# Sums of squares and residuals by adding DMA transfers instead of GpSimd additions, in an RG-LRU / gMLP / conv-FFN block

## The chip, the cores and the metric

The kernel runs on one core of a Trainium2 chip. The metric is the device time of one execution in microseconds, lower is better. Engines are named as the profile names them: PE (TensorE), DVE (VectorE), ACT (ScalarE), POOL (GpSimd), SP (SyncE, which here only issues DMA transfers).

## The reference

One residual block over 2048 positions of width 1024, in f32. A mixer and a feed-forward network each have the same frame: RMS norm, scale and shift from a conditioning vector, the layer, RMS norm, gate, residual.

```
h = rmsnorm(x, g_mix_pre) * (1 + sc_m) + sh_m
z = h @ w_in                       # lru_x | lru_gate | g_u | g_v
y_lru  = rg_lru_group(lru_x, lru_gate, ...)
y_gmlp = gmlp_group(g_u, g_v, ...)
y = concat(rmsnorm(y_lru), rmsnorm(y_gmlp)) @ w_out
x = x + gt_m * rmsnorm(y, g_mix_post)
h = rmsnorm(x, g_ffn_pre) * (1 + sc_f) + sh_f
up = causal_depthwise_conv(h @ w_up)      # width 3
y = (gelu(up_g) * up_v) @ w_down
x = x + gt_f * rmsnorm(y, g_ffn_post)
```

Each rmsnorm needs a mean of squares over the 1024 channels of a position: `x * rsqrt(mean(x*x) + EPS) * g`.

## The kernel before, in words

Channels lie on the 128 partitions (8 blocks of them), positions along the free axis. The mixer goes over four chunks c = 0 to 3 of 512 positions, the FFN over two halves C of 1024. A tile `[128, 2, 512]` (512 KB) holds two channel blocks of a chunk, so a chunk is four tiles, j = 0 to 3. Matmuls are done as three products of float32r parts (`mm3`, L177 to L179, and `prod`, L971 to L973), and `split` (L136 to L141) makes the two parts.

A mean of squares is built by the class `SumSq`: ACT squares a tile (L215), POOL adds it to the first one (L219), `done` adds the two halves on DVE (L223) and splits the sum (L140, L141); `rms_bcast` multiplies it with a matrix of 1/1024 on PE (L199), so that every partition has the mean, and ACT and DVE make the reciprocal root (L202, L203). It is used at these places:

- `x_rms` (tiles `n_s`): the norm ahead of the mixer, chunks 1 to 3, three additions each.
- `norm_scale` (`rl_s`, `rg_s`): the norms of the two halves of y, all four chunks, one addition each.
- `mixer_out` (`rp_s`): the product with `w_out`, evicted to `oo`, squared, all chunks, three additions each.
- `mixer_post` (chunks 0 and 1) and `late_post` (chunks 2 and 3), tiles `rq_s`: scale by gate and norm on DVE (L604, L583), load the chunk's x as `xr` through the pool `ld` of three buffers, add it (on POOL at L605, on DVE at L584), store to `x2d` in DRAM (SP), square, three additions each.

`late_post` runs late, beside the FFN's first products, and takes its input back from `o2d` in DRAM. Background work is written as generators in the list `bg`; `tick` advances each by one step between pieces of PE work, and `wait` inserts empty steps. All of this fixes a priority for each instruction; the framework's planner then simulates the engines (`schedule_with_timeline_sim=True`) and fixes the order of each engine's instructions. On the chip every engine, and the issuing queues of SP, ACT and POOL, run their own list in order, with semaphores between them.

Other work on POOL: weight splits in the first chunks (L141), storing split weights to DRAM (`kept`, L169, transfers issued by POOL), products in the LRU (L380, L503), and from the first FFN half on the additions that make the seven weight pieces of `up_weights` (L951 to L959, `wt`), which feed ACT and DVE splits and then PE.

Of the kernel before, what the change touches and what calls it, by code (L numbers as in the profile page):

```python
# [13 lines left out]
ALU = mybir.AluOpType  # L14
# [26 lines left out]
def block_kernel(ctx: ExitStack, tc: tile.TileContext, xt, cols, rows, wada, wada_r, win_k, win_s, win_v, wgate, wsp, wout, wup, wdown, out):  # L41
# [12 lines left out]
    vec, act, pool, pe, sync = nc.vector, nc.scalar, nc.gpsimd, nc.tensor, nc.sync  # L54

    def t4(name):
        return tp.tile([P, 2, 512], F32, tag="t4", name=name)
# [39 lines left out]
    def start(*gens):  # L97
        bg.extend(gens)
        return gens

    def wait(n):
        for _ in range(n):
            yield
# [25 lines left out]
    x2d = dram.tile([NFC, P, ND, FT], F32, name="x2d")  # L129
# [59 lines left out]
    def rms_split(ssum, name, n=512):  # L189
        with tc.high_priority(offset=100):  # L190
            shl = y4(f"{name}_hl")
            split(shl[:, 0, :n], shl[:, 1, :n], ssum, "dve")
        return shl

    def rms_bcast(shl, scale, name, tag="r2", bufs=2, n=512):

        pt = bank(f"{name}_m")
        for q in range(2):
            pe.matmul(out=pt[:, :n], lhsT=onesD, rhs=shl[:, q, :n], start=(q == 0), stop=(q == 1))  # L199
        r = rp.tile([P, 512], F32, tag="r", name=f"{name}_r")  # L200
        with tc.high_priority(offset=100):
            act.activation(out=r[:, :n], in_=pt[:, :n], func=AF.Sqrt, scale=scale, bias=epst)  # L202
            vec.reciprocal(out=r[:, :n], in_=r[:, :n])  # L203
        return r

    class SumSq:


        def __init__(self, name, eng=None):
            self.acc, self.name, self.n, self.eng = None, name, 0, eng or pool  # L210

        def add(self, t):
            s = t4(f"{self.name}_s{self.n}")
            self.n += 1
            act.activation(out=s, in_=t, func=AF.Square)  # L215
            if self.acc is None:
                self.acc = s
            else:
                self.eng.tensor_tensor(out=self.acc, in0=self.acc, in1=s, op=ALU.add)  # L219

        def done(self):
            a = self.acc
            vec.tensor_tensor(out=a[:, 0], in0=a[:, 0], in1=a[:, 1], op=ALU.add)  # L223
            return rms_split(a[:, 0], self.name)

    def load_x(src, c, j, name, mk=None):
        x = mk(f"{name}_{j}") if mk else lp.tile([P, 2, 512], F32, tag="ld", name=f"{name}_{j}")
        sync.dma_start(out=x, in_=src[c // 2, :, 2 * j:2 * j + 2, (c % 2) * 512:(c % 2) * 512 + 512])
        return x

    rx = {}
# [2 lines left out]
    def x_rms(c, late=2):  # L234
        q = SumSq(f"n{c}")
        for j in range(4):
            q.add(load_x(xt, c, j, f"xq{c}"))
            yield
        yield
        hl = q.done()  # L240
        yield from wait(late)
        rx[c] = rms_bcast(hl, 1.0, f"n{c}", "rr", 4)

    def build_h(src, c, hl, s, sh, name):
        hi, lo = hl
        r = rx[c]
        for j in range(4):
            x = load_x(src, c, j, name)
            hi.append(h4(f"{name}hi{j}"))
            lo.append(h4(f"{name}lo{j}"))  # L250
            for b in range(2):
                d = 2 * j + b
                vec.scalar_tensor_tensor(out=x[:, b], in0=x[:, b], scalar=s[:, d:d + 1], in1=r, op0=ALU.mult, op1=ALU.mult)
                act.activation(out=hi[j][:, b], in_=x[:, b], func=AF.Identity, bias=sh[:, d:d + 1])
            for b in range(2):
                d = 2 * j + b
                vec.scalar_tensor_tensor(out=lo[j][:, b], in0=x[:, b], scalar=sh[:, d:d + 1], in1=hi[j][:, b].bitcast(F32), op0=ALU.add, op1=ALU.subtract)
            yield
# [288 lines left out]
    def mixer_out(c, late=False):  # L547
        Yt = Y[c]
        O = []
        q = SumSq(f"rp{c}")  # L550
        for j in range(4):
            pt = psum(f"o{c}_{j}")
            for b in range(2):
                wh, wl = weight_once(("o", 2 * j + b), wout[2 * j + b], [P, 8, P], f"wout{c}_{j}_{b}", pool if b else vec)
                for k in range(8):
                    mm3(pt[:, b], (wh[:, k], wl[:, k]), (Yt[k // 2][0][:, k % 2], Yt[k // 2][1][:, k % 2]), k == 0, k == 7)
                tick()
            o = t4(f"oo{c}_{j}")
            act.copy(out=o, in_=pt)
            q.add(o)  # L560
            if late:
                sync.dma_start(out=o2d[c - 2, :, j], in_=o)
            else:
                O.append(o)
        return O, q
# [8 lines left out]
    def late_post(c):  # L574

        r = rlate[c]
        q = SumSq(f"rq{c}")
        for j in range(4):
            x = load_x(xt, c, j, f"xr{c}")
            o = t4(f"ol{c}_{j}")  # L580
            sync.dma_start(out=o, in_=o2d[c - 2, :, j])
            for b in range(2):
                vec.scalar_tensor_tensor(out=o[:, b], in0=o[:, b], scalar=gm[:, 2 * j + b:2 * j + b + 1], in1=r, op0=ALU.mult, op1=ALU.mult)  # L583
            vec.tensor_tensor(out=o, in0=o, in1=x, op=ALU.add)  # L584
            sync.dma_start(out=x2d[c // 2, :, 2 * j:2 * j + 2, (c % 2) * 512:(c % 2) * 512 + 512], in_=o)
            q.add(o)
            yield
        hl = q.done()
        yield
        rq[c] = hl  # L590
# [3 lines left out]
    def mixer_post(c, O, q):  # L594
        yield
        hl = q.done()
        yield from wait(2)
        r = rms_bcast(hl, 1.0, f"rp{c}")
        q = SumSq(f"rq{c}")
        for j in range(4):  # L600
            x = load_x(xt, c, j, f"xr{c}")
            for b in range(2):
                o = O[j][:, b]
                vec.scalar_tensor_tensor(out=o, in0=o, scalar=gm[:, 2 * j + b:2 * j + b + 1], in1=r, op0=ALU.mult, op1=ALU.mult)  # L604
            pool.tensor_tensor(out=O[j], in0=O[j], in1=x, op=ALU.add)  # L605
            sync.dma_start(out=x2d[c // 2, :, 2 * j:2 * j + 2, (c % 2) * 512:(c % 2) * 512 + 512], in_=O[j])
            q.add(O[j])
            yield
        yield
        hl = q.done()  # L610
        yield from wait(6)
        rx[c] = rms_bcast(hl, 1.0, f"rq{c}", "rr", 4)
# [199 lines left out]
    for c in range(1, NC):  # L812
        nt = start(mixer_norm(0) if c == 1 else norm_split(c - 1))
        xr = start(x_rms(c + 1, 8)) if c + 1 < NC else ()
        mixer_z(c)
        drain(*xr, *nt)
        if c == 1:
            m3, = start(ada_task(3, 1))
        if c == 2:
            m4, = start(ada_task(4, 1))  # L820
        if c + 1 < NC:
            ht = start(h_task(c + 1, False), norm_scale(c, 3))
            O, q = mixer_out(c - 1)
            drain(*ht)
            if c == 1:
                drain(m2)
                vec.tensor_tensor(out=gm, in0=modc[:, 16:24], in1=colr("g_mix_post", 0, 8), op=ALU.mult)
            start(mixer_post(c - 1, O, q))
# [290 lines left out]
    def late_chunks():  # L1119

        yield from late_rms(NC - 1, q3)
        for c in (NC - 2, NC - 1):
            yield
            yield from late_post(c)
            yield
            rx[c] = rms_bcast(rq[c], 1.0, f"rq{c}")
# [5 lines left out]
    O, q = mixer_out(NC - 2, True)  # L1132
# [3 lines left out]
    O, q3 = mixer_out(NC - 1, True)  # L1136
# [91 lines left out]
```

## Time and profile before

| | |
|---|---|
| median of 3 runs | 2222.09 us (2219.21 to 2222.97) |
| the profiled execution | 2222.2 us, its span 2220.4 us |
| mean granted TensorE clock | 0.971 |
| instructions | 24098 |
| mixer and `late_post` | from the start to about 950 us |
| FFN, first half `down` and second half | about 1200 us to the end |

The span runs from the first to the last instruction; the profiled execution's time is 1.8 us longer. The granted clock is a share of TensorE's full speed of 2.4 GHz; it has two levels, 1 and 0.5 (1.2 GHz), and a mean between them says how much of a stretch was spent at each. A busy time is the time in which an engine had an instruction running. An instruction that is held by something else while it runs counts as busy, and shows as a longer duration.

### The profile page before, as it was taken

To read this page: it belongs to the slowest core of one execution; us is meant where nothing else is said; L and a number is where in the kernel's file an instruction comes from. 1 tells how busy PE (TensorE), PEld (TensorE's weight loads), DVE (VectorE), ACT (ScalarE), POOL (GpSimd) and SP (SyncE) were. 2 spreads that over 40 slices of the span, in tenths; PEclk is the share of its full clock that TensorE was granted. 3 is DMA by queue.
4 is the path that set the end of the run, shared out by engine and by line. 5 is a ranking of instruction groups with operands and counts; after the bars stand their busy time and mean duration, and the time that the engine had idled before them with its cause. 6 is when DMAs were issued, how large, how long until landed. Compare 5 with 4: busy or idle time off the path is not lost.

```text
span 2220.4 us, 24098 instructions
## 1 busy us (share of the span) xinstructions
PE 2072.0 (93%) x9032; PEld 1700.7 (77%) x9032; DVE 1435.9 (65%) x1598; ACT 928.8 (42%) x1154; POOL 424.8 (19%) x248
## 2 busy tenths in 40 slices
PE   5898969999998998799999999989999999999995
PEld 4686858888877876588888888868888888888883
DVE  7788789795766887898777437474444444533634
ACT  3472733534635544355555344343233332422422
POOL 4454243234203332443320000020000000000000
PEclk9999989999999999899999999999999999999997
DMA  8587568587674887877775546537666666444541
GB/s 315 187 311 286 193 242 291 206 287 256 225 268 164 305 314 265 311 264 276 271 291 189 181 134 215 173 120 286 220 221 224 220 223 221 145 159 149 212 148 60
DMA packets 157748, 501.14 MB, mean 226 GB/s; under 512 B 15296, under 2 KB 15424, under 8 KB 157632
## 3 DMA queue, kind: packets, MB, share of 16 engines
q1 hardware_dynamic: 149568, 470.25, 59.9%
q0 software_dynamic: 6912, 25.17, 2.9%
q10 hardware_dynamic: 1152, 4.19, 0.5%
q8 instruction: 71, 1.16, 0.2%
q14 instruction: 45, 0.37, 0.1%
HBM read 343.31 MB, written 156.24 MB: 225 GB/s over the span
## 4 chain that ended last, share of the span: by engine, by line
PE 73%; DVE 14%; ACT 4%; DMA 4%; issue 4%; POOL 1%; SPq 0%; DVEq 0%; ACTq 0%; POOLq 0%
PE dn L177 8%; PE dn L178 8%; PE dn L179 8%; PE upa L973 7%; PE upa L972 7%; PE upa L971 7%; PE upc L973 3%; PE upc L972 3%; PE upc L971 3%; PE upb L973 2%; PE upb L971 2%; PE upb L972 2%; PE lg L177 1%; PE lg L178 1%; PE lg L179 1%
## 5 line engine op out<-in xcount | busy, mean ns | idle before, releaser
L177 PE MATMUL dn<-gh,wd_h 128*128 128x512 f32 x768 | 297.0, 390 | 2.9 <-ACT fr_r L202 1.6
L178 PE MATMUL dn<-gl,wd_h 128*128 128x512 f32 x768 | 296.6, 389 | 0.0
L141 DVE TENSOR_TENSOR wd_l<-wd_r,wd_h 128x1024 fp32r<-128x1024 f32 x96 | 118.0, 1230 | 231.9 <-ACT wd_h L136 216.1
L179 PE MATMUL dn<-gh,wd_l 128*128 128x512 f32 x768 | 265.0, 389 | 0.0
L136 ACT CAST wd_h<-wd_r 128x1024 fp32r<-128x1024 f32 x96 | 101.2, 1056 | 286.8 <-PE dn L178 276.1
L918 DVE SCALAR_TENSOR_TENSOR a<-Rg,prm,a 128x1023 f32<-128x1023 f32 x92 | 132.4, 1439 | 126.9 <-ACT a L916 126.7
L177 PEld LDWEIGHTS dn<-gh,wd_h 128*128 128x128 f32 x768 | 144.2, 188 | 35.4 <-ACT wd_h L136 3.0
L179 PEld LDWEIGHTS dn<-gh,wd_l 128*128 128x128 f32 x768 | 144.1, 188 | 29.8
L178 PEld LDWEIGHTS dn<-gl,wd_h 128*128 128x128 f32 x768 | 144.2, 188 | 29.8
L918 DVE SCALAR_TENSOR_TENSOR a<-Rv,prm,a 128x1023 f32<-128x1023 f32 x92 | 121.9, 1325 | 38.7 <-ACT a L916 38.5
L951 POOL TENSOR_TENSOR wt<-wuv,wug 128x512 f32<-128x512 f32 x24 | 39.3, 1637 | 523.7 <-DMA wuv<-in_wup_dram 411.7
L916 ACT ACTIVATE a<-Rv,prm 128x1024 f32<-128x1024 f32 x46 | 57.2, 1244 | 133.3 <-DVE Rv L1020 132.6
L136 ACT CAST wt<-wt 128x512 fp32r<-128x512 f32 x72 | 44.7, 622 | 113.3 <-PE upa L973 39.5
L141 DVE TENSOR_TENSOR wt<-wt,wt 128x512 fp32r<-128x512 f32 x72 | 62.7, 873 | 24.0 <-ACT wt L136 23.8
L976 ACT ACTIVATE a<-a 128x1024 f32<-128x1024 f32 x48 | 50.9, 1061 | 53.7 <-DVE a L923 31.9
L1020 DVE TENSOR_TENSOR Rv<-upa,m 128x512 f32<-128x512 f32 x46 | 31.6, 687 | 58.3 <-PE upa L973 58.3
L141 DVE TENSOR_TENSOR gl<-gr,gh 128x1024 fp32r<-128x1024 f32 x48 | 58.5, 1218 | 12.5 <-PE upa L973 6.3
L977 DVE TENSOR_TENSOR a<-a,a 128x1024 f32<-128x1024 f32 x48 | 58.8, 1225 | 2.5 <-ACT a L976 2.5
L916 ACT ACTIVATE a<-Rg,prm 128x1024 f32<-128x1024 f32 x46 | 57.2, 1243 | 4.4 <-DVE a L918 3.2
L136 ACT CAST gh<-gr 128x1024 fp32r<-128x1024 f32 x48 | 50.8, 1058 | 13.3 <-DMA gr<-gd 6.1
L1024 ACT COPY Rg<-upa 128x512 f32<-128x512 f32 x46 | 26.8, 584 | 69.7 <-PE upa L973 69.7
L959 POOL TENSOR_TENSOR wt<-wug,wt 128x512 f32<-128x512 f32 x24 | 39.9, 1662 | 82.4 <-DVE wt L141 55.5
(583 smaller groups left out, 5738.5 us busy)
## 6 DMA issues: line engine op xcount, KB each, us to landing
wd_r<-in_wdown_dram SPq DMA_DIRECT2D x96, 512.0 KB, 4.4
wkd<-wt SPq DMA_DIRECT2D x88, 512.0 KB, 4.0
wkd<-w SPq DMA_DIRECT2D x66, 512.0 KB, 3.7
w<-wkd SPq DMA_DIRECT2D x66, 512.0 KB, 4.3
gd<-a SPq DMA_DIRECT2D x48, 512.0 KB, 3.9
gr<-gd SPq DMA_DIRECT2D x48, 512.0 KB, 3.5
wrt<-wkd SPq DMA_DIRECT2D x44, 512.0 KB, 4.3
wt<-wkd SPq DMA_DIRECT2D x44, 512.0 KB, 4.6
```

Source lines behind the costliest of these rows:

```text
L136: act.copy(out=hi, in_=src)
L141: (leng or vec).tensor_tensor(out=lo, in0=src, in1=hi.bitcast(F32), op=ALU.subtract)
L177: pe.matmul(out=out, lhsT=wh, rhs=mh, start=first, stop=False)
L178: pe.matmul(out=out, lhsT=wh, rhs=ml, start=False, stop=False)
L179: pe.matmul(out=out, lhsT=wl, rhs=mh, start=False, stop=last)
L916: act.activation(out=a, in_=R, func=AF.Identity, scale=w[2], bias=col("ffn_conv_b", blk))
L918: vec.scalar_tensor_tensor(out=a[:, s:], in0=R[:, :FT - s], scalar=w[t], in1=a[:, s:], op0=ALU.mult, op1=ALU.add)
L971: pe.matmul(out=pt, lhsT=wh, rhs=mh, start=first and not more and k == 0, stop=False, skip_group_check=more)
L972: pe.matmul(out=pt, lhsT=wh, rhs=ml, start=False, stop=False, skip_group_check=more)
L973: pe.matmul(out=pt, lhsT=wl, rhs=mh, start=False, stop=last and k == 3, skip_group_check=more)
L976: act.activation(out=g, in_=g, func=AF.Gelu_apprx_tanh)
L977: vec.tensor_tensor(out=g, in0=g, in1=v, op=ALU.mult)
```

## The change

The additions of `SumSq` are no longer POOL instructions: POOL issues a DMA transfer from the tile of squares to the accumulator that adds to what is there (`accum_op`). The residual of `mixer_post` (on POOL) and of `late_post` (on DVE) becomes a transfer too, which reads x from DRAM and adds it to the tile, so that the load of `xr` and its buffer go. `part` only names a slice that stood in full before.

```diff
     class SumSq:
-        def __init__(self, name, eng=None):
-            self.acc, self.name, self.n, self.eng = None, name, 0, eng or pool
+        def __init__(self, name):
+            self.acc, self.name, self.n = None, name, 0
         def add(self, t):
             ...
-                self.eng.tensor_tensor(out=self.acc, in0=self.acc, in1=s, op=ALU.add)
+                pool.dma_start(out=self.acc, in_=s, accum_op=ALU.add)
 
+    def part(src, c, j):
+        return src[c // 2, :, 2 * j:2 * j + 2, (c % 2) * 512:(c % 2) * 512 + 512]
...
     def late_post(c):
         for j in range(4):
-            x = load_x(xt, c, j, f"xr{c}")
             o = t4(f"ol{c}_{j}")
             ...
-            vec.tensor_tensor(out=o, in0=o, in1=x, op=ALU.add)
-            sync.dma_start(out=x2d[c // 2, :, 2 * j:2 * j + 2, (c % 2) * 512:(c % 2) * 512 + 512], in_=o)
+            pool.dma_start(out=o, in_=part(xt, c, j), accum_op=ALU.add)
+            sync.dma_start(out=part(x2d, c, j), in_=o)
             q.add(o)
...
     def mixer_post(c, O, q):
         for j in range(4):
-            x = load_x(xt, c, j, f"xr{c}")
             ...
-            pool.tensor_tensor(out=O[j], in0=O[j], in1=x, op=ALU.add)
-            sync.dma_start(out=x2d[c // 2, :, 2 * j:2 * j + 2, (c % 2) * 512:(c % 2) * 512 + 512], in_=O[j])
+            pool.dma_start(out=O[j], in_=part(xt, c, j), accum_op=ALU.add)
+            sync.dma_start(out=part(x2d, c, j), in_=O[j])
             q.add(O[j])
```

## Rows read from the trace of the kernel before

**Rows 1.** The page: busy time by engine, and the chain that ended last, by engine.

```profile
PE 2072.0 (93%) x9032; PEld 1700.7 (77%) x9032; DVE 1435.9 (65%) x1598; ACT 928.8 (42%) x1154; POOL 424.8 (19%) x248
...
PE 73%; DVE 14%; ACT 4%; DMA 4%; issue 4%; POOL 1%; SPq 0%; DVEq 0%; ACTq 0%; POOLq 0%
```

**Rows 2.** Stretches: start:end, length, busy us (instructions), clock, DMA share, GB/s.

```profile
500.00:600.00 100.00, 99.10 (x457) 82.32 (x456) 64.73 (x76) 54.18 (x64) 34.49 (x14) 1.00 0.64 225
...
285.00:330.00 45.00, 26.87 (x113) 21.88 (x112) 37.34 (x31) 18.00 (x21) 24.24 (x15) 0.77 0.72 257
...
780.00:950.00 170.00, 141.95 (x560) 112.01 (x560) 145.74 (x149) 75.36 (x105) 68.96 (x35) 0.92 0.78 288
```

**Rows 3.** PE's waits up to 1200 us: total us, times, longest.

```profile
PE o L177 <- DVE modc L285: 18.1, 1, 18.1
...
PE rl_m L199 <- DVE rl_hl L140: 7.3, 1, 7.3
...
PE rq_m L199 <- DVE rq_hl L140: 5.6, 2, 3.0
```

**Rows 4.** POOL's groups by line: count, busy us, mean ns, idle before.

```profile
L219 POOL TENSOR_TENSOR rp_s<-rp_s,rp_s 128x1024 f32<-128x1024 f32 x12 | 31.6, 2630 | 117.7 <-ACT rp_s L215 117.6
L219 POOL TENSOR_TENSOR rq_s<-rq_s,rq_s 128x1024 f32<-128x1024 f32 x12 | 31.2, 2596 | 44.4 <-ACT rq_s L215 44.3
...
L219 POOL TENSOR_TENSOR n_s<-n_s,n_s 128x1024 f32<-128x1024 f32 x9 | 23.6, 2622 | 16.6 <-ACT n_s L215 16.5
L605 POOL TENSOR_TENSOR oo<-oo,xr 128x1024 f32<-128x1024 f32 x8 | 21.6, 2697 | 34.9 <-DVE oo L604 33.0 <-DMA xr<-in_xt_dram 1.9
...
L219 POOL TENSOR_TENSOR rg_s<-rg_s,rg_s 128x1024 f32<-128x1024 f32 x4 | 10.4, 2599 | 6.5 <-ACT rg_s L215 6.5
L219 POOL TENSOR_TENSOR rl_s<-rl_s,rl_s 128x1024 f32<-128x1024 f32 x4 | 9.6, 2396 | 3.5 <-ACT rl_s L215 3.5
```

**Rows 5.** Timeline, DVE and POOL: start us, duration us, what.

```profile
311.23 0.68 DVE L223 TENSOR_TENSOR rl_s<-rl_s 128x512 f32<-128x512 f32 x1
...
118.02 2.88 DVE L223 TENSOR_TENSOR n_s<-n_s 128x512 f32<-128x512 f32 x1
...
300.42 7.77 DVE L257 SCALAR_TENSOR_TENSOR x2lo<-x,modc,x2hi 128x512 fp32r<-128x512 f32 x1
...
300.68 2.36 POOL L219 TENSOR_TENSOR rl_s<-rl_s,rl_s 128x1024 f32<-128x1024 f32 x1
```

**Rows 6.** Transfers: issues with median us to landing; issue times in ns.

```profile
kept_v<-winv_h POOLq DMA_DIRECT2D x4, 512.0 KB, 4.3
...
kept_s<-win_l POOLq DMA_DIRECT2D x12, 512.0 KB, 7.4
...
L169 POOL DMA_DIRECT2D kept_s<-win_h x12 | 7.0, 582 | 19.5 <-ACT win_h L136 19.5
...
L228 SPq DMA_DIRECT2D xr<-in_xt_dram x16: 383/406/1751, 342.8 to 892.1; - x16
```

**Rows 7.** Timeline at the last chunk's norm.

```profile
590.78 2.88 POOL L219 TENSOR_TENSOR rg_s<-rg_s,rg_s 128x1024 f32<-128x1024 f32 x1 [4.65 <-ACT rg_s L215]
...
595.00 0.47 PE L199 MATMUL rg_m<-rg_hl,onesD 128*128 128x512 f32 x1 [0.90 <-DVE rg_hl L140]
```

**Rows 8.** `late_post`: DVE's group L584, timeline at the chunks' ends, ACT's wait.

```profile
L584 DVE TENSOR_TENSOR ol<-ol,xr 128x1024 f32<-128x1024 f32 x8 | 9.7, 1215 | 0.1
...
833.28 2.38 POOL L219 TENSOR_TENSOR rq_s<-rq_s,rq_s 128x1024 f32<-128x1024 f32 x1
...
841.75 0.68 DVE L223 TENSOR_TENSOR rq_s<-rq_s 128x512 f32<-128x512 f32 x1
...
929.04 2.37 POOL L219 TENSOR_TENSOR rq_s<-rq_s,rq_s 128x1024 f32<-128x1024 f32 x1
...
933.05 0.68 DVE L223 TENSOR_TENSOR rq_s<-rq_s 128x512 f32<-128x512 f32 x1
...
ACT rq_s L215 <- DVE ol L584: 17.1, 7, 4.8
```

More of the change, by code (lines that the diff above doesn't have):

```diff
@@ L224, in done @@
             return rms_split(a[:, 0], self.name)
+    def part(src, c, j):
+        return src[c // 2, :, 2 * j:2 * j + 2, (c % 2) * 512:(c % 2) * 512 + 512]
     def load_x(src, c, j, name, mk=None):
         x = mk(f"{name}_{j}") if mk else lp.tile([P, 2, 512], F32, tag="ld", name=f"{name}_{j}")
-        sync.dma_start(out=x, in_=src[c // 2, :, 2 * j:2 * j + 2, (c % 2) * 512:(c % 2) * 512 + 512])
+        sync.dma_start(out=x, in_=part(src, c, j))
         return x
```

## The prediction

> **What bounds the kernel now.** I read the page first: TensorE is busy 93% of the span, and the chain that ended last is 73% PE and 14% DVE [rows 1]. So the question is where PE stands still, and for whom. The table by stretches answers where. In 500 to 600 us PE is busy 99.1 of 100 us: whatever becomes faster there is worth nothing. In 285 to 330 us it is busy 26.9 of 45 us, and in 780 to 950 us 142 of 170; the granted clock falls to 0.77 and 0.92 there, and DVE is busy 83% and 86% [rows 2]. PE's waits then say for whom: one wait of 18.1 us for the DVE reduction that frees a PSUM bank (`modc`, L285), one of 7.3 us for the cast of `rl_hl`, two of 5.6 us together for the cast of `rq_hl` [rows 3]. All of these end on DVE. Before the FFN's second half this kernel is a TensorE kernel with a crowded VectorE beside it. A reader should keep apart two prices: what an edit does to DVE's queue, and how late a sum of squares arrives at the small matmul (L199) that stands in PE's queue.
>
> **What is removed.** The GpSimd additions: 12 of `rp_s`, 12 of `rq_s`, 9 of `n_s`, 4 each of `rg_s` and `rl_s`, which is 41 additions of squares, and 8 residuals `oo`: 31.6 + 31.2 + 23.6 + 10.4 + 9.6 + 21.6 = 128.0 us of POOL [rows 4]. POOL is 19% busy, so its own time buys nothing. What they do to DVE does. The 512-column addition L223 takes 0.68 us in the clear and 2.88 us beside a running POOL addition, and one DVE operation that overlaps a run of three POOL additions took 7.77 us, starting 0.26 us before the `rl_s` addition at 300.68 [rows 5]. So an addition on POOL can hold DVE for its whole length, 2.2 us or more: at most 49 x 2.2 = 108 us of DVE, and 0 if none meets DVE work. DVE is over 80% busy in the stretches that matter, so most meet some.
>
> Where PE already runs full this is free time for nobody. Three places count.
>
> Term 1, 285 to 330 us. The 7.77 us operation stands in DVE's queue directly ahead of the L285 reduction that PE awaits. Without the `rl_s` and `rg_s` additions (2.36 us and a mean of 2.60) it ends about 5.0 us earlier; the third of the run, a weight split on POOL, stays. The wait of 18.1 us becomes 13. The clock loss of this stretch is 0.23 x 45 = 10.4 us; in proportion 5.0/18.1 of it, 2.9 us, comes back. Together -7.9 us.
>
> Term 2, 780 to 950 us. The eight DVE residuals L584 of `late_post` go: 8 x 1.215 = 9.7 us [rows 8]. Its six `rq_s` additions stop holding DVE: at most 13 us, I take half, 6.5. That is 16.2 us off a DVE that is busy 146 of 170 us, while PE loses 28 us. Not all of it is on PE's path; I take two thirds, -10.8 us (bounds 0 and -22.7). The granted clock costs 0.08 x 170 = 13.6 us there; a third of the lost time saved gives back about -4 us.
>
> **What is added: 57 transfers on POOL's queue.** Of each I need the issue and the landing. The nearest rows are the kernel's own POOL transfers of 512 KB: an issue takes POOL 0.58 us, and they land 4.3 us (`winv_h`) to 7.4 us (`win_l`) after it [rows 6]. 57 x 0.58 = 33 us of POOL in place of 128. No row shows a transfer that adds. It must also read its destination, so the lower bound of its landing is 4.3 us and the upper twice 7.4, 14.8 us. I take 7.0, near the loaded plain row, since at the 288 GB/s of the late stretch [rows 2] 512 KB are 1.8 us, so that most of a landing in these rows is not the moving of bytes.
>
> The Trainium skill (DMA: Bandwidth & Descriptors, section on the anatomy of one DMA on the gpsimd path) fits a landing as a constant of some 2.0 us plus the bytes over 436 GB/s; that is an estimate of 3.2 us for 512 KB. The rows of this loaded kernel are above it in every case, 4.3 to 7.4 us, so the sum does not go by it; by it the time would be that of the third rival below or a little less.
>
> Each sum therefore takes 7.0 us instead of about 2.5 for its last addition, and the additions of one sum follow each other, since each needs the one before it landed. Who waits: POOL itself, in order, between two additions of one sum (behind it the weight pieces `wt`, the products L503 and L380); DVE, in order, at L223; PE at L199. Most have slack or fall where PE has work queued. The exposed ones:
>
> Term 3, last chunk's norm. The `rg_s` addition starts at 590.78, takes 2.88 us, and PE waits for its result at 595.00 for 0.90 us already [rows 7]. With a landing of 7.0 us: +4.1 us. At the first chunk's wait of 7.3 us [rows 3] the later landing (+4.5) stands against two operations on `rl_hl` and `rg_hl` that are held 2.2 us each; I put 0 there (bounds -4 and +5).
>
> Term 4, ends of `late_post`. Now the last residual lands after 7.0 us instead of 1.2, its square follows, and the last addition lands after 7.0 instead of 2.4: +10.4 us for each of two chunks. The slack between the end of the addition and DVE's L223 is 841.75 - 835.66 = 6.1 us for chunk 2 and 933.05 - 931.41 = 1.6 us for chunk 3 [rows 8]. Unplanned that is 4.3 + 8.8 = 13.1 us, and PE's waits on `rq_hl` grow by it. But the instruction order is drawn up by a planner that knows that a transfer takes time, and it can put L199 behind more `up` products. Between 0 and 13.1 I take half, +6.5.
>
> Term 5, squares and stores behind the residual. ACT waited 17.1 us in 7 waits for `ol` already [rows 8]; each could be 5.8 us longer, 41 us, if nothing were planned around it, and behind the square stand the copies that free PE's banks. SP's store to `x2d` waits as well, with weight loads behind it; against that SP loses 16 loads of 0.41 us each [rows 6] and their buffers in the pool `ld`. ACT has 95 of 170 us idle. I take +3 (bounds 0 and +23). In `mixer_post` (370 to 540 us) the same waits lie under a full PE: nothing, and if that cover went, up to 8 x 4.3 = 34 us of ACT.
>
> Term 6, bytes. In 780 to 950 us 288 GB/s x 170 us = 49 MB move at a DMA share of 0.78. The 6 additions there and, if reading the destination counts, all 14 transfers once more, add 3 to 10 MB: a share of 0.83 to 0.94. I take +1 (bounds 0 and +6).
>
> Sum: -7.9 - 10.8 - 4 + 4.1 + 6.5 + 3 + 1 = -8.1 us. The profiled execution took 2222.2 us (span 2220.4), 0.1 us from the median of the three runs. 2222.2 - 8.1 = 2214.
>
> **Rivals.** (a) Slower: the landing decides. Its place is the end of each `late_post` chunk and the `rg_s` of the last chunk, its price 1 us per us of landing at five links (one in term 3, two in each chunk of term 4). At 7.0 us with no help from the planner the losses are 4.1 + 13.1 + 3 + 1 = 21, against gains of 22.7: from a little above that landing it goes over. At 10 us: 7.1 + 25.1 + 6 + 1 = 39, less 22.7, is +16.5; three waits of 8 to 15 us would also cost clock, at the 10.4 us for 18 us above some 5 us each for two of them. About 2247. For it: the DMA share of 0.78, and additions that must follow each other. Against: the slack of 6.1 us, the planner.
> (b) No change, 2222: the losses at these links eat what DVE gains. For it: PE is full in most of the mixer and the terms are all small against 2222.
> (c) The landings are short, 4.3 us, like the quickest row. Then term 3 is +1.4, term 4 is 0 + 3.4 halved to 1.7, term 5 is nothing: -22.7 + 1.4 + 1.7 + 1 = -18.6, 2204. For it: the quickest POOL row; against it: the other rows, up to 7.4.
>
> **How the numbers follow.** A measurement here can tell about 0.2%, 4.4 us, from no change. Forecast (-8) 0.34, (c) 0.14, (b) 0.17, (a) 0.35. So faster 0.48, same 0.17, slower 0.35. All gains at their bounds with short landings give some -35, all losses at theirs +55; leaving out a tenth on either side, between (c) less the wider bound of term 2 and (a), I get 2190 to 2250. The forecast's own range is 2206 to 2218.
>
> **What would show it.** Right: L223 and L257 on DVE near 0.7 us where the additions were; the wait at L285 down to about 13 us; POOL near 330 us busy; the new transfers landing in 6 to 8 us; PE busy above 145 us in the stretch of `late_post`. Wrong: landings over 10 us; PE's waits at L199 for `rq_hl` or `rg_hl` over 8 us each; ACT's waits for `ol` above 40 us; SP's stores to `x2d` holding the weight loads. What would upset all of it is a different order of PE's work from the planner, since every small wait here depends on what was placed ahead of it.

## The result, and the profile after

The changed kernel takes 2296.59 us (2296.08 to 2299.52, four runs) where the kernel before took 2222.53 on the same chip: a ratio of 1.0337 [1.0319, 1.0355], slower by 74 us. The forecast was 2214 in a range of 2190 to 2250; the time lies outside it, on the slow side. The profiled execution took 2296.5 us, its span 2294.7. Two executions among the runs below are left out of the medians, one of run 1 (5918 us) and one of run 13 (11856 us); that of run 1 was the profiled one, so run 1 has a time but no stretches and waits.

The page of the changed kernel: busy time by engine, the queue of POOL's transfers (packets, MB, share of 16 engines' span).

```profile
PE 2083.3 (91%) x9032; PEld 1708.8 (74%) x9032; DVE 1361.0 (59%) x1590; ACT 926.4 (40%) x1155; POOL 352.7 (15%) x256
...
q0 software_dynamic: 17168, 55.06, 9.7%
```

Beside [rows 1]: DVE is busy 75 us less, POOL 72 us less, and PE 11 us longer for the same 9032 matmuls. Both engines got their relief and the time still grew: of the 74 us PE stands still for 63 and is busy for 11 more.

Two moments cut the span into parts that can be compared although the order of the work moved: the first product `up` and the first product `dn` of the FFN, read from the rows of these tiles. Before, `up` starts at 681.9 us and `dn` at 1186.3. In the changed kernel they start at 718.3 and 1259.0. Up to `up` (the mixer) 36 us are lost, from `up` to `dn` (the late part, in which `late_post` runs) another 36: 540.7 us in place of 504.4. Behind `dn` the two differ by less than 2 us. The same columns as in [rows 2], first for the two parts of the kernel before:

```profile
95.00:682.00 587.00, 544.04 (x2432) 448.63 (x2430) 450.52 (x481) 290.52 (x342) 208.99 (x115) 0.97 0.72 257
...
682.00:1186.00 504.00, 475.95 (x2029) 388.39 (x2030) 412.05 (x445) 249.24 (x349) 164.96 (x96) 0.97 0.75 274
```

and for the changed kernel, with the two stretches of [rows 2] behind them in which PE stood still before:

```profile
95.00:718.00 623.00, 555.50 (x2437) 455.79 (x2435) 401.74 (x486) 292.38 (x344) 142.12 (x114) 0.94 0.82 271
...
718.00:1259.00 541.00, 475.94 (x2030) 389.62 (x2031) 387.01 (x434) 246.08 (x350) 160.55 (x104) 0.93 0.77 263
...
285.00:330.00 45.00, 33.95 (x142) 27.49 (x141) 38.97 (x44) 17.31 (x22) 18.91 (x14) 0.85 0.81 271
...
780.00:950.00 170.00, 136.87 (x582) 110.95 (x581) 116.13 (x125) 68.99 (x99) 56.23 (x35) 0.90 0.83 276
```

In the late part PE is busy for as long as before (475.9 us) and idle 65 us in place of 28. In the mixer it is idle 67 us in place of 43, and busy 11 us longer, at a granted clock of 0.94 in place of 0.97. The stretch of 285 to 330 us did get better, as forecast: PE 34 of 45 us in place of 27 (at the same times, not quite at the same work, since the changed kernel is some 5 us later there).

PE's waits in the changed kernel up to 1300 us (total, times, longest), beside [rows 3]:

```profile
PE upc L972 <- ACT m L1009: 37.6, 4, 23.0
...
PE up L972 <- ACT oo L562: 15.4, 1, 15.4
...
PE o L177 <- DVE modc L288: 11.0, 1, 11.0
...
PE lg L177 <- DMA win_h<-kept_s: 10.3, 1, 10.3
...
PE rq_m L199 <- DVE rq_hl L140: 9.3, 1, 9.3
PE n_m L199 <- DVE n_hl L140: 9.2, 1, 9.2
...
PE rl_m L199 <- DVE rl_hl L140: 6.3, 1, 6.3
...
PE rg_m L199 <- DVE rg_hl L140: 3.1, 1, 3.1
```

Two waits of the kernel before that [rows 3] doesn't show:

```profile
PE up L971 <- ACT oo L559: 7.8, 1, 7.8
...
PE upc L971 <- ACT m L1008: 5.5, 1, 5.5
```

The wait for `modc` fell from 18.1 to 11.0 us. But the largest is now one that was 5.5 us in one wait before: the ACT copy `m` that empties a PSUM bank of the FFN's `upc` product, 37.6 us in four. No addition and no sum stands in that row. In the mixer PE's idle time grew by 24 us, and the rows say where most of it stands: 10.3 us for the weights of `lg`, 9.2 for the sum `n_m`, 7.6 more ahead of `up`, 2.2 more for `rg_m`, against 8.1 less for `modc` and `rl_m`. The other 11 us of the mixer are the busier PE at the lower clock.

POOL's transfers by tile: KB each, median us from issue to landing, beside [rows 6].

```profile
rp_s<-rp_s POOLq DMA_DIRECT2D x12, 512.0 KB, 8.6
rq_s<-rq_s POOLq DMA_DIRECT2D x12, 512.0 KB, 8.6
n_s<-n_s POOLq DMA_DIRECT2D x9, 512.0 KB, 9.7
oo<-in_xt_dram POOLq DMA_DIRECT2D x8, 512.0 KB, 11.8
ol<-in_xt_dram POOLq DMA_DIRECT2D x8, 512.0 KB, 9.8
...
rl_s<-rl_s POOLq DMA_DIRECT2D x4, 512.0 KB, 9.6
rg_s<-rg_s POOLq DMA_DIRECT2D x4, 512.0 KB, 10.3
```

All are above the 7.0 us taken. What one of them holds up is seen in the timeline of the changed kernel in `late_post` (start, duration, what, in brackets the idle time before and its releaser; the first row is the square of the tile before):

```profile
853.47 1.06 ACT L215 ACTIVATE rq_s<-ol 128x1024 f32<-128x1024 f32 x1 [8.05 <-DMA ol<-in_xt_dram]
...
867.33 1.22 POOL L586 DMA_DIRECT2D ol<-in_xt_dram  x1 [3.49 <-DVE ol L585]
...
867.85 0.82 SPq L930 DMA_DIRECT2D wuv<-in_wup_dram  x1
...
877.02 0.37 SPq L587 DMA_DIRECT2D x2d<-ol  x1
877.08 1.06 ACT L215 ACTIVATE rq_s<-ol 128x1024 f32<-128x1024 f32 x1 [13.86 <-DMA ol<-in_xt_dram]
878.04 0.57 ACT L1009 COPY m<-upc 128x512 f32<-128x512 f32 x1
878.50 0.91 POOL L219 DMA_DIRECT2D rq_s<-rq_s  x1 [9.95 <-ACT rq_s L215]
...
878.66 0.79 PE L972 MATMUL upc<-hs_00h,w 128*128 128x512 f32 x1 [23.02 <-ACT m L1009]
...
880.28 3.75 DVE L919 SCALAR_TENSOR_TENSOR a<-Rv,prm,a 128x1023 f32<-128x1023 f32 x2 [9.63 <-ACT a L917]
```

A reader should follow one landing through five queues. POOL issues the residual of `ol` at 867.33 and it lands near 877. ACT stands 13.9 us at the square of `ol`, which is next in its order; the copy `m` behind it, which needs nothing of the residual, runs at 878.04. SP issues nothing from 867.85 on, with the store of `ol` next. POOL stands 9.95 us for the square, DVE 9.63 for ACT, and PE 23.0 us for the bank that `m` frees. Not all of this is one landing. PE stands from 855.6 us on, 11.7 us ahead of the issue, when ACT was late already by the 8.05 us that it had stood at the square before, and 4.1 of ACT's 13.9 us lie ahead of the issue too. So the 23 us hold parts of two landings.

The wait for `lg` in the mixer is of the same kind, by SP's queue (a row of several issues has their times together):

```profile
391.37 6.14 SPq L607 DMA_DIRECT2D x2d<-oo  x3
...
398.71 0.95 SPq L164 DMA_DIRECT2D win_h<-kept_s  x1
...
410.87 0.80 PE L177 MATMUL lg<-x2hi,win_h 128*128 128x512 f32 x1 [10.33 <-DMA win_h<-kept_s]
```

SP stood 11.0 us for the residual of `oo` ahead of these stores, and the weights that PE awaits were issued behind them. They then took 12 us to land (7 for the issue at 393.45 us in the kernel before), with the DMA engines full, at a share of 0.99 in 375 to 400 us: the order of the queue and the load both have a part.

ACT's waits of the first kind, and DVE's at L223 for the last addition of a sum (all stretches, so that some rows of one tile sum several chunks):

```profile
ACT rq_s L215 <- DMA ol<-in_xt_dram: 58.0, 7, 13.9
...
DVE rq_s L223 <- DMA rq_s<-rq_s: 30.8, 2, 17.0
DVE rp_s L223 <- DMA rp_s<-rp_s: 18.7, 4, 9.5
DVE n_s L223 <- DMA n_s<-n_s: 16.2, 2, 8.3
DVE rl_s L223 <- DMA rl_s<-rl_s: 10.9, 3, 4.1
DVE rg_s L223 <- DMA rg_s<-rg_s: 7.4, 2, 6.2
```

58.0 us for ACT against 17.1 before [rows 8], and 84.0 us for DVE in 13 waits, each of which holds what stands behind it in DVE's queue; 77.5 of them lie in the mixer.

### The profile page after: what moved, and what is told of

Read it like the earlier page. It is cut to its first block, busy times and chain, and to the rows that moved or that the text cites. A ratio compares the mean times of both kernels' runs of the same rounds, so it can differ in the third digit from the quotient of the medians.

```text
span 2294.7 us, 24096 instructions
## 1 busy us (share of the span) xinstructions
PE 2083.3 (91%) x9032; PEld 1708.8 (74%) x9032; DVE 1361.0 (59%) x1590; ACT 926.4 (40%) x1155; POOL 352.7 (15%) x256
## 4 chain that ended last, share of the span: by engine, by line
PE 57%; DMA 5%; DVE 4%; issue 3%; ACT 1%; POOL 1%; SPq 0%; DVEq 0%; ACTq 0%; POOLq 0%
PE dn L177 8%; PE dn L178 7%; PE dn L179 7%; PE upa L972 6%; PE upa L974 6%; PE upa L973 6%; PE upc L974 3%; PE upc L972 3%; PE upc L973 3%; DMA ol<-in_xt_dram 2%; PE upb L972 2%; PE upb L974 2%; PE upb L973 2%; DVE a L919 1%; PE up L972 1%
## 5 line engine op out<-in xcount | busy, mean ns | idle before, releaser
L280 DVE SCALAR_TENSOR_TENSOR ada_m<-wada,cact,ada_m 128x1024 f32<-128x1024 f32 x28 | 46.3, 1655 | 22.4 <-DMA wada<-in_wada_r_dram 22.4
```

## The experiments

Three theories stood once the result was known, in this order. The landings (W in the expectations): a wait for one does the harm, through the instructions behind the one that waits. The load (B): 57 more transfers, each read, added and written, slow the others. The order (P): taking the additions from POOL was worth little, and another order of the work makes the loss. The table has every run; `up` is the first product `up` in us, late the us from there to the first `dn`, both of the profiled execution; each ratio is against before on the chip of that run (2220.4 to 2223.0 us).

| run | median us | ratio [95%] | `up` | late |
|---|---|---|---|---|
| before | 2222.53 | 1 | 681.9 | 504.4 |
| after | 2296.59 | 1.0337 [1.0319, 1.0355] | 718.3 | 540.7 |
| 1 squares alone | 2246.15 | 1.0102 [1.0083, 1.0121] | | |
| 2 residuals alone | 2262.78 | 1.0182 [1.0165, 1.0199] | 686.2 | 541.2 |
| 3 no addition | 2190.8 | 0.9858 [0.9838, 0.9877] | 666.1 | 482.8 |
| 4 plain copies | 2245.83 | 1.0108 [1.0085, 1.0131] | 684.2 | 523.0 |
| 5 one step later | 2288.65 | 1.0311 [1.029, 1.0332] | 709.7 | 538.2 |
| 6 `late_post` residual | 2263.63 | 1.0198 [1.0181, 1.0215] | 680.0 | 540.4 |
| 7 DVE adds squares | 2211.58 | 0.996 [0.9946, 0.9975] | 674.9 | 501.9 |
| 8 before and load | 2253.86 | 1.0151 [1.0134, 1.0167] | 711.8 | 508.4 |
| 9 after, three steps | 2219.87 | 0.999 [0.9976, 1.0003] | 713.3 | 474.1 |
| 10 squares, later `done` | 2229.57 | 1.0038 [1.0028, 1.0048] | 699.0 | 493.6 |
| 11 runs 9 and 10 | 2235.83 | 1.0078 [1.005, 1.0106] | 705.9 | 497.3 |
| 12 DVE adds all | 2212.72 | 0.9961 [0.9949, 0.9974] | 668.4 | 502.0 |
| 13 before, three steps | 2197.77 | 0.9889 [0.9865, 0.9914] | 682.1 | 483.0 |
| 14 DVE in mixer, steps | 2180.1 | 0.9816 [0.9793, 0.9839] | 671.6 | 473.6 |
| 15 run 12, steps | 2187.41 | 0.9846 [0.9824, 0.9869] | 669.6 | 482.7 |
| 16 free DRAM load | 2300.53 | 1.0356 [1.0335, 1.0377] | 758.4 | 504.1 |
| 17 load behind additions | 2250.49 | 1.0127 [1.0111, 1.0144] | 707.4 | 507.1 |
| 18 no one waits | 2205.49 | 0.9926 [0.9912, 0.9941] | 668.0 | 500.8 |

**Runs 1, 2 and 3: the parts, and the work left out.** Run 1 is after with the residuals of before, run 2 before with the 16 residuals of after, run 3 before with

```
-                self.eng.tensor_tensor(out=self.acc, in0=self.acc, in1=s, op=ALU.add)
+                pass
```

> Only the 41 additions of squares by adding transfers; residuals as in the kernel before. Theory W (waits in order): what costs is that an instruction that needs a transfer's landing (9 to 12 us in the changed kernel) holds everything behind it on its in-order engine, above all ACT's squares behind the residual's landing; then the residuals carry more than half of the 74 us and this run is +20 to +35 us. Theory B (bytes): what costs is the DMA engines' time, about 2.8 us for an adding transfer against 1.3 for a plain one; the squares carry 41 x 2.8 = 115 us of it and the residuals only 16 x 1.4 = 22, so this run is +55 to +65 us.

> Only the 16 residuals by adding transfers; additions of squares on POOL as before. Theory W: +35 to +55 us, with ACT's waits for the residual near the 58 us (ol) and 39 us (oo) of the changed kernel, and PE's waits on ACT's copies (L1009 or its neighbours) near 38 us. Theory B: +8 to +15 us.

> The kernel before with the 41 POOL additions of squares left out (each mean of squares then takes the first tile alone, the squares are still computed). It shows what taking them off POOL and DVE is worth when nothing takes their place. My prediction's gain for this part, terms 1 and 2 without the eight DVE residuals, is some 14 to 18 us: 2205 to 2208. If POOL's hold on DVE hides behind PE everywhere, under 5 us. If it is worth much more than I thought, 30 us and up.

24 us for the squares and 41 for the residuals, each against before on its chip (2221.9), are 65 of the 74 us. Both lie in the ranges that the landings gave (20 to 35, 35 to 55), and outside those of the load (55 to 65, 8 to 15). PE's wait for the weights of `lg`, 10.3 us in after, is 0.7 in run 2, so it may be part of the 9 us that are missing. Nearly all of the residuals' loss lies in the late part (541 against 504; the mixer 686 against 682). Run 3 ends the first half of the third theory: without the additions (the sums are then short of three tiles in four, or one in two) 31 us are gained, more than the forecast hoped for; in the profiled execution, which is 6 us quicker than the median, 16 in the mixer and 22 in the late part.

**Run 4: the same transfers as plain copies.** Each `accum_op=ALU.add` is taken out of after, so that sums and residuals are overwritten; in the two traces every engine has the same instructions in the same order.

> The changed kernel with its 57 adding transfers made plain copies of the same tiles (the sums and residuals are then overwritten, not added to); queues, waits and number of transfers stay. Theory W: a plain transfer lands in about 5 to 7 us instead of 9 to 12, so some 40 percent of the wait goes: +35 to +50 us. Theory B: half of the added DMA time goes: +25 to +37 us, with the share of the POOL queue near 5 percent. A third theory P (the planner's new order of instructions is itself worse, landings aside): +60 to +74 us with landings at 5 to 7 us.

The loss is 24 us in place of 74: the mixer is back to 684, the late part is 523. In the trace of run 4 (transfers, then waits) the landings are 1.3 to 3.1 us shorter (three of the seven tiles are shown) and the wait of ACT for `ol` and of PE for `m` shrink with them, and stay:

```profile
rq_s<-rq_s POOLq DMA_DIRECT2D x12, 512.0 KB, 7.0
...
oo<-in_xt_dram POOLq DMA_DIRECT2D x8, 512.0 KB, 8.9
ol<-in_xt_dram POOLq DMA_DIRECT2D x8, 512.0 KB, 7.8
...
ACT rq_s L215 <- DMA ol<-in_xt_dram: 38.5, 7, 11.1
...
PE upc L972 <- ACT m L1009: 29.8, 3, 18.2
```

Since the order is the same, another order doesn't explain the 50 us between this run and after; of the 24 us that stay it might have a part. Transfers that land 1.3 to 3.1 us later, and take the DMA engines longer, cost 50 us over the kernel. The run doesn't part landings from load: both fell together, and 24 us is below what either theory expected (35 to 50, 25 to 37).

**Runs 5 and 6: where the residual costs.** Run 5 is after with the store and the square one step later, run 6 before with the residual of `late_post` alone by an adding transfer.

```
             pool.dma_start(out=o, in_=part(xt, c, j), accum_op=ALU.add)
+            yield
             sync.dma_start(out=part(x2d, c, j), in_=o)
             q.add(o)
-            yield
```

> The changed kernel with the square and the store of each residual tile written one step of the background list later, so that the planner places other ACT and SP work between the adding transfer and what needs its landing. Transfers, bytes and additions are the same. Theory W (waits in order): ACT's waits for ol and oo fall from 58 + 39 us to under 40 together, PE's waits on ACT's copies from 38 + 8 us to under 20, and 20 to 40 of the 74 us come back. Theory B (bytes): under 10 us come back. P (the planner's order as such): anything, without a link to these waits.

> The kernel before with only the 8 residuals of late_post by adding transfers (mixer_post's residuals and all additions of squares stay on POOL). All 16 residuals gave +40 us. Theory W: late_post runs beside the up products, where ACT's copies free PE's banks, and mixer_post under a full PE: this run has +25 to +40 us. Theory B: bytes count alike in both places: half, +15 to +22 us.

Run 6 is run 2 (2263.6 against 2262.8): the eight residuals of `late_post` carry the whole loss of the sixteen, and `mixer_post`'s cost nothing as long as the squares are no transfers. Its trace has the same row, ACT's wait for `ol`:

```profile
ACT rq_s L215 <- DMA ol<-in_xt_dram: 70.8, 8, 13.9
...
PE upc L970 <- ACT m L1007: 41.9, 4, 22.6
```

One step in run 5 gives 8 us, where the landings had expected 20 to 40 and the load under 10. ACT still waits 41.7 us for `ol` in 8 waits, so one background step doesn't cover a landing, and PE's wait for `m` did not fall (42.7 us).

**Runs 9, 11 and 13: three steps between.** In `late_post`, empty background steps stand between residual and square, and ahead of the reduction (run 9, on after). Run 13 has the same steps in the kernel before, with no adding transfer. Run 11 adds the moves of `done()` of run 10.

```
             pool.dma_start(out=o, in_=part(xt, c, j), accum_op=ALU.add)
+            yield from wait(3)
             sync.dma_start(out=part(x2d, c, j), in_=o)
...
+        yield from wait(3)
         hl = q.done()
```

> The changed kernel with three empty background steps in late_post between the adding transfer and the store and square that need it, and three ahead of the sum's end. One step was not enough (ACT still waited 42 us for ol, and 6 of 74 us came back). Theory W: ACT's waits for ol fall under 15 us, the stretch from the first up product to the first dn product goes from 541 us back to 500 to 512 (504 before), and the time to 2255 to 2268. Theory B or P: the stretch stays over 530 us.

> The kernel before, with three empty steps in late_post between the residual (on DVE, as before) and the store and square, and three ahead of the sum's end; no adding transfer. If the late gain is the spacing's: the stretch from first up to first dn product is 475 to 490 us instead of 504, and the time -15 to -30 us. If it is that DVE lost eight residuals and six holds: 500 to 506, and within 4 us of before.

> The whole change with both moves. Theory W throughout: 2205 to 2230. W in late_post and B in the mixer: 2238 to 2255. Neither: over 2270.

The late part of run 9 as one stretch:

```profile
713.00:1187.00 474.00, 468.87 (x2052) 386.56 (x2052) 400.85 (x438) 245.20 (x348) 171.24 (x104) 0.99 0.86 303
```

and that of run 13:

```profile
682.00:1165.00 483.00, 470.99 (x2053) 386.93 (x2054) 429.18 (x449) 244.71 (x348) 177.74 (x96) 0.99 0.79 290
```

Run 9 gives back 77 us: the late part falls from 541 to 474 with every adding transfer still there and more bytes per second (303 GB/s). PE is idle 5 us of 474, and ACT's waits have no row for `ol` left. The landings had expected a late part of 500 to 512, the load over 530: that shows the first theory for the late part. But run 13 is the control that a reader should not leave out: the steps alone are worth 24 us to the kernel before. Its `late_post` had the same fault in small, ACT's 17.1 us for `ol` [rows 8]. Of run 9's late part only the 9 us between 483 and 474 belong to the adding transfers. Run 11 shows that spacing is no rule of its own: with `done()` moved as well the late part is 497, and PE waits 21.2 us in it, six times, for DVE (`upa` for `Rv`), which run 9 has at 2.9. What delays DVE there was not followed.

**Runs 8, 16, 17 and 18: the load.** Run 8 is before with 82 plain transfers from SBUF to DRAM beside the additions, two for each:

```
+                for t in range(2):
+                    pool.dma_start(out=dram.tile([P, 2, 512], F32, name=...), in_=s)
```

In run 16 they go from DRAM to DRAM and hang on nothing, in run 17 the same are tied behind the addition. In run 18 each addition is replaced by an adding transfer of a piece of x into the tile `s`, which no one reads, so that the sums are as short as in run 3.

> The kernel before, and beside each of the 41 additions two plain 512 KB transfers from the tile of squares to DRAM, which nothing waits for: 82 x about 1.4 us of DMA engine time, as much as 41 adding transfers take, without any landing on a path. Theory B (bytes and engine time): +20 us and up. Theory W: under +10 us, of which some is POOL's 82 x 0.58 us of issuing.

> The kernel before, and beside each of the 41 additions two 512 KB transfers from the input x to unused DRAM, issued by POOL: the same load and issues as in the run with added load (+33 us, 30 of them in the mixer), but no tile is held. Theory B (the DMA engines' time by itself slows the mixer): +20 us and up. Theory W (the earlier run's loss came from tiles of squares held until the transfers had read them): under +10 us.

> As the run with DRAM to DRAM load, each pair of transfers now tied behind its addition on POOL, so that the load falls where the adding transfers fall and holds no tile. Theory B in the mixer: first up product at 700 us or later (before 682), total +20 us and up. Theory W: under 690 us, total under +10 us.

> The kernel before with each of the 41 additions replaced by an adding transfer of x from DRAM into the tile of squares just made, which nothing reads afterwards: the mean of squares takes the first tile alone, as in the run without additions (2190.8 us, first up product at 666 us). Same number of adding transfers in the same places, no landing awaited by DVE or by the next transfer. Theory W in the mixer: 2188 to 2200 us, first up product under 676 us. Theory B: 2210 us and up, first up product at 690 us or later.

Run 16 doesn't answer: its transfers were all issued in the first 157 us. Runs 8 and 17 lose 30 and 25 us in the mixer, none to speak of later; by them load alone could make most of the mixer's loss. But they keep POOL's additions and give it 82 issues besides: POOL is busy 248 and 258 us in their mixers, in place of 209 before, and no wait of PE there ends on a transfer. POOL's queue is a rival to the load in these two, which no run parts. Run 18 says the opposite: its mixer has a DMA share of 0.87, above after's 0.82, and loses 2 us to run 3's (668 against 666). The stretch of the mixer in run 18:

```profile
95.00:668.00 573.00, 538.29 (x2420) 444.10 (x2418) 408.18 (x482) 288.01 (x340) 163.02 (x112) 0.98 0.87 291
```

and in run 3:

```profile
95.00:666.00 571.00, 539.79 (x2427) 446.38 (x2425) 410.20 (x482) 289.38 (x341) 123.08 (x81) 0.98 0.74 264
```

The landings in run 18 are as long as after's (11.5 us for `n_s`). So adding transfers that nobody waits for cost the mixer nothing; in after somebody waits. Its late part is 18 us longer than run 3's, which is load or POOL's issues; no run parts these. For the mixer's 36 us, the first theory has run 18 for it, and the second 8 and 17, if POOL's queue isn't what they show; run 4 takes them away under either.

**Runs 7, 10, 12, 14 and 15: towards a better kernel.** Run 10 is run 1 with each `done()` some steps later. In run 7 DVE adds the squares, in run 12 the residual of `mixer_post` too; run 15 is run 12 with the steps of run 13; run 14 is run 15 with `late_post`'s residual and squares by adding transfers.

```
-                self.eng.tensor_tensor(out=self.acc, in0=self.acc, in1=s, op=ALU.add)
+                vec.tensor_tensor(out=self.acc, in0=self.acc, in1=s, op=ALU.add)
```

> Only the squares by adding transfers (+22 us as such), with the end of each sum (DVE's addition L223, which needs the last landing) some background steps later; the place of the matmul L199 stays where it was in the mixer. Theory W in the mixer: DVE's waits at L223 (some 80 us in the changed kernel) mostly go and with them the loss: -10 to +8 us against the kernel before. Theory B in the mixer (weights and tiles arrive later since the DMA engines are busy; the run that only added load lost 33 us): +15 us or more stay.

> The kernel before with the 41 additions of squares on DVE, where one takes about 1.22 us (50 us in all), in place of 2.5 us on POOL. Leaving them out gave -31 us, so POOL's hold on DVE costs PE something like that. If DVE's time is what PE waits for, 50 us of DVE against the hold that goes: -5 to +10 us. If the hold is worse than its length (DVE starves while POOL runs one after the other): -10 to -20 us.

> The 41 additions of squares and the 8 residuals of mixer_post on DVE, none on POOL and no adding transfer. The squares alone gave -9 us. Eight residuals more are 8 x 1.2 = 10 us of DVE against 8 x 2.7 = 22 us in which POOL can hold it, in a stretch where PE is nearly full: -12 to -4 us against the kernel before. Slower than the squares alone if DVE's own time there reaches PE.

> As the run with all additions on DVE, with the three empty steps in late_post and no adding transfer at all. If the spacing is what gains in the late stretch: 2180 to 2195, like the run with adding transfers there; if the transfers are: 2205 to 2213, no better than without the steps.

> Mixer's additions and residuals on DVE (668 us up to the first up product in the run that had all on DVE), and in late_post alone the adding transfers for residual and squares with three empty steps (474 us from there to the first dn product). If the two parts add up: 2205 - 28 = 2177, between 2172 and 2190, faster than both kernels. If the late gain was tied to the mixer's late end: over 2195.

Run 10 gains 17 us on run 1 and is 7.9 us over before, at the upper edge of what the landings expected (8, the load 15 or more); its mixer is still at 699, 17 us behind. Runs 7 and 12 gain 9 us each on before: DVE takes the additions at less than what POOL's additions cost it. With the steps it is 2187.4, and with adding transfers in `late_post`, where the steps cover the landing, 2180.1: 42 us better than before (0.9816 [0.9793, 0.9839]) and 116 better than after. The two parts of run 14:

```profile
95.00:671.00 576.00, 538.61 (x2421) 444.92 (x2420) 441.87 (x522) 287.83 (x339) 98.57 (x71) 0.97 0.73 261
...
671.00:1145.00 474.00, 467.92 (x2053) 386.25 (x2054) 400.83 (x441) 246.15 (x348) 163.74 (x102) 0.99 0.85 301
```

## Why the prediction was wrong

**The step that failed is term 5**, "squares and stores behind the residual", taken as +3 with an upper bound of 23. It saw the mechanism (the square waits for the landing, and "behind the square stand the copies that free PE's banks") and then leaned on a planner that would put other work between, and on ACT's idle time of 95 us in 170. Its own figure for the case in which nothing is planned around the landing, 41 us for ACT, is what came: ACT's waits for `ol` grew from 17.1 to 58.0 us. The planner put too little work between, and ACT's idle time was no cover, since the copies for PE stand behind the square: run 6, which is the residual of `late_post` alone, costs 43 us (2263.6 against 2220.4 on its chip). PE's wait for `m` grew by 32 us (5.5 to 37.6), almost the 36 us of the late part, and run 9, with steps between, has no such wait and a late part of 474 us. The bound was wrong too: it priced ACT's waits alone, where the same landing also stopped SP's loads, POOL and DVE. In `mixer_post` the term had nothing, under a full PE; there the store behind the landing has a part in PE's 10.3 us at `lg`.

**The second is one clause on the sums**, "Most have slack or fall where PE has work queued". DVE waits 84 us at L223, and PE 9.2 us at a sum (`n_m`) that the forecast doesn't list. The squares cost 24 us by themselves (run 1), where run 3 says that taking them from POOL should give 31. That is a swing of some 55 us. Of the causes the waiting is shown by run 18, where the same number of adding transfers without a reader costs the mixer 2 us; what part the load has stays open.

**The landing** was taken as 7.0 us, between 4.3 and 14.8; it measured 8.6 to 11.8. The prediction's four signs of being wrong all came: landings over 10 us (`oo`, `rg_s`), a wait for `rq_hl` over 8 us (9.3), ACT's waits for `ol` above 40 us (58.0), and SP's stores ahead of weights that PE awaited. By the Trainium skill (DMA: Bandwidth & Descriptors, section on the anatomy of one DMA on the gpsimd path) 512 KB would land in an estimated 3.2 us; the plain copies of run 4 (6.8 to 8.9 us) are at two to three times that and the adding transfers at about three, and the measurement decides.

**Term 1** was right in kind and low in size: the wait for `modc` fell by 7.1 us, not 5.0, PE gained 7.1 busy us in the stretch, and the clock rose from 0.77 to 0.85. The operation that took 7.77 us [rows 5] is one of eight on this tile; the longest of the eight takes 0.75 us in the changed kernel (below: both kernels, shortest, median and longest in ns). The 2.88 us of [rows 5] were misread: what ran on POOL beside that row is the split of the weight `win_l` (117.75 us, 2.60 us long), which the change leaves, and not an addition. The Trainium skill (SBUF — State Buffer, section on its two separate sides) has DVE operations with two inputs in SBUF and GpSimd operations that read SBUF exclude each other for a whole instruction; the trace agrees, 7.77 against 0.75, and goes further, since DVE there sat out three POOL operations in a row.

```profile
L257 DVE SCALAR_TENSOR_TENSOR x2lo<-x,modc,x2hi x8: 721/742/7774, 281.7 to 316.9; 128x512 fp32r<-128x512 f32 x8
...
L260 DVE SCALAR_TENSOR_TENSOR x2lo<-x,modc,x2hi x8: 721/744/747, 294.9 to 329.3; 128x512 fp32r<-128x512 f32 x8
```

**Term 2** (-10.8 and -4 of clock in the late part) can't be read from after, where the waits cover it. Run 3 shows the share of the squares, 22 us of the late part, above the 15 forecast for all. **Term 3** was +4.1; PE's wait for `rg_m` grew by 2.2 us (0.90 to 3.1). **Term 4** was +6.5; the waits for `rq_m` grew by 3.7 (5.6 to 9.3). **Term 6**, the bytes, was +1: the DMA share in 780 to 950 us rose from 0.78 to 0.83, inside its bounds, and no run of this case prices that alone. `mixer_post`'s residuals cost nothing by themselves (run 6 beside run 2).

**Rival (a)**, that the landing decides, was the right one: at 10 us it gave 2247. It counted the five links at L199, and those came out small. Of the 50 us that it lacked the rows show the queues behind the waiting instructions, 32 us at `m` and 10.3 at `lg`; what the load adds in the mixer is open.

## What to carry to other kernels

An instruction that waits for a transfer stops everything behind it on its engine (13.9 us of ACT, 11.0 of SP above): before an addition is moved from an engine to a transfer, list what stands next in each queue that reads the result, and price the landing once for each of them. Put work of the landing's length between the transfer and its reader (three background steps here, 77 us, though the steps of run 11 did less) and try the same spacing without the change, since that control alone was worth 24 us. Where several additions follow each other into one sum, an engine that is busy 65% (DVE) was still the better place than a transfer: 2211.6 against 2246.2 us.

## What the runs showed of the hardware

An adding transfer takes twice the transfer time of a plain one. POOL's queue is busy 2.9% of 2220.4 us for 48 plain transfers, 64 us on all 16 engines, 1.34 us each. After has 57 more and 9.7% of 2294.7 us: 158 us more, an estimated 2.8 us each. In run 4, the same as plain copies, the queue is at 6.4% of 2242.6 us, an estimated 1.4 us each. Its landing is 1.3 to 3.1 us longer in the same order of work (after against run 4, above).

POOL's issue of one takes 0.90 us from SBUF and 1.22 us from DRAM, in the rows of the changed kernel by line (count, busy, mean ns, idle before); the same two as plain copies, in run 4, take 0.56 and 0.74 us:

```profile
L219 POOL DMA_DIRECT2D rq_s<-rq_s x12 | 10.7, 895 | 88.8 <-ACT rq_s L215 64.0 <-DMA rq_s<-rq_s 24.9
...
L586 POOL DMA_DIRECT2D ol<-in_xt_dram x8 | 9.8, 1221 | 27.3 <-DVE ol L585 11.5 <-DVE ftails L921 7.0 <-DVE w L141 4.9
```

The 24.9 us in the first row are POOL's waits for the addition before into the same tile. The Trainium skill (DMA: Bandwidth & Descriptors, rules for kernel authors) asks for that wait, as an adding transfer reads its destination and writes it later; here it is three waits of up to 11.1 us.

In run 16 82 free DRAM to DRAM transfers brought the first 200 us to 399 and 373 GB/s, and PE to 38 and 56 busy us of 100, where it was 64 and 92 before. PE's largest wait there is 53.5 us for a weight split on POOL (`wk_wlo`), whose first piece ran at 53.4 us, behind 27 of these transfers in POOL's queue; POOL issued one each 2.4 us or so. The weights themselves landed later too (`wk_r` 19.9 us in place of 9.5), so no run parts queue and load here either.
